# Input projection: the low parts of every other weight unit on GpSimd, and split weights in all units

## The chip, the cores and the metric

The kernel runs on one core of a Trainium2 chip. The metric is the device time of one execution in microseconds (us); lower is better. Engines are named as the profile names them: PE is TensorE's matmul, PEld its weight load, DVE is VectorE, ACT is ScalarE, POOL is GpSimd, SP is SyncE, which issues most DMAs. Data lies in SBUF (tiles named `raw`, `wh`, `wl`, `macc`, `big` and so on) or in PSUM (tiles named `ps`), where PE writes its sums.

## The reference

One decoder layer over 256 tokens of 2048 features in float32: a modulated RMSNorm, a mixer (gated short convolution beside gated linear attention, GLA) and a gated feed-forward part, each with a residual. The change lies in the first product of the mixer, the input projection `h @ w_in`:

```
mod = (c_act @ w_mod[l] + b_mod[l])[:, None, :]
sh_m, sc_m, g_m, sh_f, sc_f, g_f = jnp.split(mod, 6, axis=-1)
h = rmsnorm(x, mix_pre_w[l]) * (1 + sc_m) + sh_m
proj = h @ w_in                                   # (256, 2048) @ (2048, 6160)
cb, cc, cx, q, k, v, r, a_lr = jnp.split(proj, splits, axis=-1)
```

The last 16 columns, `a_lr`, have a path of their own. The other 6144 columns are 48 tiles of 128.

## The kernel before, in words

**Split products.** PE multiplies operands of type fp32r at a short time each and float32 operands at a longer one. To keep the precision of float32, each weight block `raw` is split in two fp32r tiles: ACT copies it into the high part `wh` (`high`, line 138, the copy at line 140), and DVE subtracts that from the block to make the low part `wl` (`low`, line 143, the subtraction at line 145). The activations are split in the same way. A product is then three matmuls: high by high, high by the activation's low part, low by high (lines 490, 491, 492).

**Whole weights.** A unit whose number stands in `FULL`, `FULL1`, `FULL2` or `PLAIN` does without the split: PE multiplies `raw` by the unsplit activations in float32, one matmul for each product (line 487). Before the change these are units 5, 9 and 13 of the last chunk (`FULL`, line 44).

**Chunks and units.** The 16 tiles of the contraction are cut into chunks of 2, 4, 5 and 5 (`CHUNKS`, line 25), so that the projection can begin before the whole modulation is there. In each chunk `in_units` (line 450) makes a list of units of work. In chunks 0 and 1 there are 12 units of 4 column tiles. In chunks 2 and 3 there are 18: units 0 to 3, 6 to 11, 15 and 16 have 3 column tiles, units 4, 5, 12, 13, 14 and 17 have 2. A unit's weight block is 128 partitions by 2048 elements in chunk 1, and by 1920 (3 tiles) or 1280 (2 tiles) in chunks 2 and 3. A unit has `prep` (the load of `raw`, issued by SP, and ACT's high part), `lows` (DVE's low part), `mm` (the matmuls) and `fin`, which adds the finished PSUM banks to the projection's tiles on DVE (`evac`, line 405; line 416, and line 414 by the helper at line 136 for q).

**The order.** `drive` (line 69) writes out the order of all units, and every engine runs its own instructions in that order. While unit i is multiplied, `prep` of unit i+2 and `lows` of unit i+1 have just been issued; then come the sums of unit i-1. `raw` has 6 buffers, `wh` and `wl` have 3 each (`NRAW`, `NHI`, `NLO`, lines 47 to 49). Between these steps stand the steps of the modulation (`mod_steps`, line 157): SP loads a slice of `w_mod`, and DVE multiplies it by a scalar and adds it to an accumulator (line 184, by the helper at line 136). The first step of each accumulator has POOL clear it (line 170) and load the bias row (line 171); it stands ahead of `prep` in unit 9 of chunk 1 (for chunk 3's modulation), in unit 7 of chunk 2 (the mixer's gate) and in unit 4 of chunk 3 (for the feed-forward part). From the last chunk on, the steps of the linear attention stand between the units too; on DVE they are among others lines 611 to 627, 647 and 668.

**POOL.** Before the change it clears accumulators, issues small loads, turns the masks into bytes (line 250, in unit 2 of chunk 2) and adds two residual pieces at the end (line 925).

Of the kernel before, what the change touches and what calls it, by code (L numbers as in the profile page):

```python
# [6 lines left out]
F32 = mybir.dt.float32  # L7
F32R = mybir.dt.float32r
# [6 lines left out]
P = 128  # L15
# [10 lines left out]
PLAIN = ()  # L26
# [14 lines left out]
CONV = (9, 12, 13, 15)  # L41
MODS = (10, 21, 31, 46, 70)
F2_AT = (70, 75, 16)
FULL = (5, 9, 13)
FULL1 = ()
FULL2 = ()
NRAW = 6
NHI = 3
NLO = 3
# [54 lines left out]
def layer_kernel(ctx: ExitStack, tc, x, c, w_mod, b_mod, mix_pre_w, mix_post_w, w_in, conv_w, gate_w2, gate_b,  # L104
                 gla_norm_w, w_out, ffn_pre_w, ffn_post_w, w_up, ffn_conv_w, w_down, ident_in, masks_in, out):
    nc = tc.nc
# [6 lines left out]
    wts = ctx.enter_context(tc.tile_pool(name="wts", bufs=2))  # L113
# [5 lines left out]
    def nm(s):  # L119
        uid[0] += 1  # L120
        return f"{s}_{uid[0]}"
# [4 lines left out]
    def bank(shape):  # L126
        return psp.tile(shape, F32, tag="ps", name=nm("ps"))
# [4 lines left out]
    def raw_tile(shape):  # L132
        return wts.tile(shape, F32, tag="raw", name=nm("raw"), bufs=NRAW)
# [4 lines left out]
    def high(raw, shape):  # L138
        hi = wts.tile(shape, F32R, tag="wh", name=nm("wh"), bufs=NHI)
        nc.scalar.copy(hi, raw)  # L140
        return hi

    def low(raw, hi, shape):
        lo = wts.tile(shape, F32R, tag="wl", name=nm("wl"), bufs=NLO)
        nc.vector.tensor_sub(lo, raw, hi.bitcast(F32))  # L145
        return lo

# [189 lines left out]
    def rstd_of(ss, n, name):  # L337
        r = std_of(ss, n, name)
        nc.vector.reciprocal(r, r)
        return r  # L340
# [9 lines left out]
    def norm_squares(t, name):  # L350
        ss = small.tile([P, 4], F32, tag=name + "ss", name=nm(name))
        for h in range(4):
            square_sum(xs[t][h // 2][:, (h % 2) * 512:(h % 2 + 1) * 512], ss[:, h:h + 1])
        return ss
# [50 lines left out]
    def evac(ci, pair, ps):  # L405

        name = names[pair // 2]
        if name not in proj:
            proj[name] = slot([P, 4, T])
        dst = proj[name][:, (pair % 2) * 2:(pair % 2) * 2 + 2, :]  # L410
        if ci == 0:
            nc.scalar.activation(dst, ps, AF.Copy, scale=QS if name == "q" else 1.0)
        elif name == "q":
            stt(dst, ps, QS, dst)
        else:
            nc.vector.tensor_add(dst, dst, ps)  # L416
# [33 lines left out]
    def in_units(ci):  # L450
        k0, n = bounds[ci], CHUNKS[ci]
        if n <= 4:
            groups = [tuple(range(g, g + 4)) for g in list(range(24, 48, 4)) + list(range(0, 24, 4))]
        else:
            groups = [tuple(range(g, g + 3)) for g in (24, 27, 30, 33)] + [(36, 37), (38, 39)]
            for o, m in ((0, 3), (3, 3), (6, 2)):
                groups += [tuple(range(g + o, g + o + m)) for g in (8, 16, 0)]
            groups += [(40, 41, 42), (43, 44, 45), (46, 47)]
        banks = {}

        def unit(tiles, plain):
            m = len(tiles)
            cur = {}

            def prep():
                r = raw_tile([P, n, m * P])
                nc.sync.dma_start(r, w_in[k0 * P:(k0 + n) * P, tiles[0] * P:(tiles[-1] + 1) * P]
                                  .rearrange("(k p) n -> p k n", p=P))
                cur["w"] = (r,) if plain else (high(r, [P, n, m * P]),)
                cur["r"] = r  # L470

            def lows():
                if not plain:
                    cur["w"] += (low(cur["r"], cur["w"][0], [P, n, m * P]),)

            def mm():
                w = cur["w"]
                for o, nt in enumerate(tiles):
                    if nt // 2 not in banks:
                        banks[nt // 2] = bank([P, 2, T])  # L480
                    ps = banks[nt // 2][:, nt % 2, :]
                    cs = slice(o * P, (o + 1) * P)
                    for kk in range(n):
                        k = k0 + kk
                        st, sp = kk == 0, kk == n - 1
                        if plain:
                            nc.tensor.matmul(ps, w[0][:, kk, cs], h32[ci][k], start=st, stop=sp)  # L487
                        else:
                            ht = hts[k // 2]
                            nc.tensor.matmul(ps, w[0][:, kk, cs], ht[:, k % 2, 0, :], start=st, stop=False)  # L490
                            nc.tensor.matmul(ps, w[0][:, kk, cs], ht[:, k % 2, 1, :], start=False, stop=False)  # L491
                            nc.tensor.matmul(ps, w[1][:, kk, cs], ht[:, k % 2, 0, :], start=False, stop=sp)  # L492

            def fin():
                for nt in tiles:
                    if nt % 2 == 1:
                        evac(ci, nt // 2, banks[nt // 2])

            return Unit(prep, lows, mm, [fin])

        return [unit(g, i in (PLAIN, FULL1, FULL2, FULL)[ci]) for i, g in enumerate(groups)]


    mts = {}
# [252 lines left out]
    def out_units(nh):  # L757
# [5 lines left out]
        def unit(k2):  # L763
# [9 lines left out]
            def lows():  # L773
                cur["w"] += (low(cur["r"], cur["w"][0], [P, 2, 1024]),)
# [89 lines left out]
    def up_units(og, ks, mode):  # L864
# [4 lines left out]
        def unit(k0):  # L869
# [8 lines left out]
            def lows():  # L878
                cur["w"] += (low(cur["r"], cur["w"][0], [P, 4, 512]),)
# [123 lines left out]
    for j, f in enumerate(steps0):  # L1003
# [5 lines left out]
        if j in NLD:  # L1009
            t = NLD.index(j)  # L1010
            r = rstd_of(norm_squares(t, f"n1{t}"), 4, f"n1{t}")
# [12 lines left out]
    for f in modulate_chunk(0, ash, early):  # L1024
        f()

    chunks = [in_units(ci) for ci in range(len(CHUNKS))]
    outs = [out_units(nh) for nh in range(2)]
    owait = outs[0] + outs[1]
# [6 lines left out]
    for ci in range(1, len(CHUNKS)):  # L1036
        n, us = CHUNKS[ci], chunks[ci - 1]
# [312 lines left out]
```

## Time and profile before

| what | value |
|---|---|
| median of 3 runs | 1216.56 us (1216.52 to 1217.66) |
| the profiled execution's own time | 1216.94 us |
| its span, first to last instruction | 1215.1 us |
| time of that execution outside the span | 1.84 us |
| granted TensorE clock, mean | 0.997 |
| chunk 1 of the projection | 76.9 to 151.8 us |
| chunk 2 | 151.8 to 244.2 us |
| chunk 3 | 244.2 to 358.4 us |

The profile gives for each engine its busy time, the groups of its instructions with their number and mean duration, the idle time ahead of them and what ended it. A row of the timeline has start, duration, engine, line, operation, output and inputs. Matmuls overlap in PE's pipeline, so the step from one start to the next is what a matmul costs, not its duration. One float32 matmul of line 487 is shown as two records.

### The profile page before, as it was taken

To read this page: it belongs to the slowest core of one execution; us is meant where nothing else is said; L and a number is where in the kernel's file an instruction comes from. 1 tells how busy PE (TensorE), PEld (TensorE's weight loads), DVE (VectorE), ACT (ScalarE), POOL (GpSimd) and SP (SyncE) were. 2 spreads that over 40 slices of the span, in tenths; PEclk is the share of its full clock that TensorE was granted. 3 is DMA by queue.
4 is the path that set the end of the run, shared out by engine and by line. 5 is a ranking of instruction groups with operands and counts; after the bars stand their busy time and mean duration, and the time that the engine had idled before them with its cause. 6 is when DMAs were issued, how large, how long until landed. Compare 5 with 4: busy or idle time off the path is not lost.

```text
span 1215.1 us, 17130 instructions
## 1 busy us (share of the span) xinstructions
PE 1178.0 (97%) x7003; PEld 1040.8 (86%) x7003; DVE 946.2 (78%) x968; ACT 570.4 (47%) x662; POOL 34.7 (3%) x52
## 2 busy tenths in 40 slices
PE   2999999999999999999999999999999999999997
PEld 1999999999997888888888888888888888888885
DVE  5899999999999886984598979698876665444463
ACT  5563422443474446444554545544544543433452
POOL 2000020000001001000000000000000000000000
PEclk9999999999999999999999999999999999999999
DMA  9999899996699886996667767767664665555522
GB/s 305 386 385 388 310 360 391 398 346 213 201 339 368 321 339 222 361 347 218 237 208 242 257 227 235 251 221 267 223 229 155 239 252 182 207 180 201 194 84 70
DMA packets 128046, 320.73 MB, mean 264 GB/s; under 512 B 8341, under 2 KB 35685, under 8 KB 118240
## 3 DMA queue, kind: packets, MB, share of 16 engines
q1 hardware_dynamic: 125360, 312.63, 72.5%
q0 software_dynamic: 2320, 6.94, 1.6%
q8 instruction: 55, 0.90, 0.3%
q14 instruction: 23, 0.19, 0.0%
q10 hardware_dynamic: 288, 0.07, 0.0%
HBM read 315.42 MB, written 4.19 MB: 263 GB/s over the span
## 4 chain that ended last, share of the span: by engine, by line
PE 91%; DVE 4%; DMA 3%; issue 1%; ACT 1%; SPq 0%; DVEq 0%; ACTq 0%
PE ps L897 27%; PE ps L899 14%; PE ps L753 9%; PE ps L754 9%; PE ps L755 9%; PE ps L490 6%; PE ps L492 6%; PE ps L491 6%; DMA raw<-in_w_mod_dram 2%; PE ps L585 1%; PE ps L487 1%; DVE wl L145 1%; PE ps L282 1%; DVE big L136 1%; DVE macc L136 1%
## 5 line engine op out<-in xcount | busy, mean ns | idle before, releaser
L140 ACT CAST wh<-raw 128x2048 fp32r<-128x2048 f32 (+3 forms) x202 | 366.1, 1815 | 507.7 <-PE ps L897 195.3
L145 DVE TENSOR_TENSOR wl<-raw,wh 128x2048 fp32r<-128x2048 f32 (+3 forms) x202 | 437.1, 2166 | 141.8 <-ACT wh L140 141.8
L897 PE MATMUL ps<-big,wh 128*128 128x512 f32 x1400 | 494.8, 398 | 0.0
L899 PE MATMUL ps<-big,wl 128*128 128x256 f32 x1400 | 393.2, 281 | 1.1 <-DVE wl L145 1.1
L897 PEld LDWEIGHTS ps<-big,wh 128*128 128x128 f32 x1400 | 263.0, 188 | 64.7
L899 PEld LDWEIGHTS ps<-big,wl 128*128 128x128 f32 x1400 | 264.5, 189 | 1.5 <-DVE wl L145 1.5
L492 PE MATMUL ps<-big,wl 128*128 128x256 f32 x733 | 209.8, 286 | 2.7 <-DVE wl L145 2.7
L490 PE MATMUL ps<-big,wh 128*128 128x256 f32 x733 | 211.4, 288 | 0.2 <-ACT wh L140 0.2
L491 PE MATMUL ps<-big,wh 128*128 128x256 f32 x733 | 209.4, 286 | 0.0
L136 DVE SCALAR_TENSOR_TENSOR macc<-raw,c_act,macc 128x2048 f32<-128x2048 f32 (+1 forms) x96 | 199.2, 2075 | 3.0 <-DMA raw<-in_w_mod_dram 2.8
L753 PE MATMUL ps<-wh,big 128*128 128x512 f32 x456 | 178.4, 391 | 0.0
L754 PE MATMUL ps<-wl,big 128*128 128x512 f32 x456 | 177.5, 389 | 0.0
L755 PE MATMUL ps<-wh,big 128*128 128x512 f32 x456 | 177.5, 389 | 0.0
L492 PEld LDWEIGHTS ps<-big,wl 128*128 128x128 f32 x733 | 142.6, 195 | 3.6 <-DVE wl L145 3.6
L490 PEld LDWEIGHTS ps<-big,wh 128*128 128x128 f32 x733 | 142.7, 195 | 2.7 <-ACT wh L140 1.4
L491 PEld LDWEIGHTS ps<-big,wh 128*128 128x128 f32 x733 | 142.8, 195 | 0.1
L755 PEld LDWEIGHTS ps<-wh,big 128*128 128x128 f32 x456 | 85.6, 188 | 17.9
L754 PEld LDWEIGHTS ps<-wl,big 128*128 128x128 f32 x456 | 85.6, 188 | 17.9 <-issue 0.2
L753 PEld LDWEIGHTS ps<-wh,big 128*128 128x128 f32 x456 | 85.6, 188 | 17.9 <-issue 0.2
L136 DVE SCALAR_TENSOR_TENSOR big<-big,fcw,big 128x254 f32<-128x254 f32 (+1 forms) x176 | 72.1, 474 | 0.0
L823 DVE TENSOR_TENSOR big<-big,ps 128x256 f32<-128x256 f32 x88 | 31.1, 415 | 48.4 <-ACT big L821 48.4
L416 DVE TENSOR_TENSOR big<-big,ps 128x512 f32<-128x512 f32 x66 | 43.1, 676 | 0.6 <-PE ps L492 0.5
(199 smaller groups left out, 668.9 us busy)
## 6 DMA issues: line engine op xcount, KB each, us to landing
raw<-in_w_up_dram SPq DMA_DIRECT2D x88, 1024.0 KB, 5.4
raw<-in_w_mod_dram SPq DMA_DIRECT2D x64, 1024.0 KB, 6.8
raw<-in_w_down_dram SPq DMA_DIRECT2D x44, 1024.0 KB, 4.8
raw<-in_w_in_dram SPq DMA_DIRECT2D x24, 960.0 KB, 8.1
raw<-in_w_mod_dram SPq DMA_DIRECT2D x32, 640.0 KB, 7.3
raw<-in_w_out_dram SPq DMA_DIRECT2D x16, 1024.0 KB, 6.9
raw<-in_w_in_dram SPq DMA_DIRECT2D x12, 1024.0 KB, 8.2
raw<-in_w_mod_dram SPq DMA_DIRECT2D x22, 512.0 KB, 6.9
```

The costliest lines, as they stand in the source:

```text
L136: nc.vector.scalar_tensor_tensor(o, a, s, b, op0=op0, op1=op1)
L140: nc.scalar.copy(hi, raw)
L145: nc.vector.tensor_sub(lo, raw, hi.bitcast(F32))
L416: nc.vector.tensor_add(dst, dst, ps)
L490: nc.tensor.matmul(ps, w[0][:, kk, cs], ht[:, k % 2, 0, :], start=st, stop=False)
L491: nc.tensor.matmul(ps, w[0][:, kk, cs], ht[:, k % 2, 1, :], start=False, stop=False)
L492: nc.tensor.matmul(ps, w[1][:, kk, cs], ht[:, k % 2, 0, :], start=False, stop=sp)
L753: nc.tensor.matmul(ps, a[:, i, 0, ts_], w[0][:, kk, ns], start=st, stop=False)
L754: nc.tensor.matmul(ps, a[:, i, 0, ts_], w[1][:, kk, ns], start=False, stop=False)
L755: nc.tensor.matmul(ps, a[:, i, 1, ts_], w[0][:, kk, ns], start=False, stop=sp)
L897: nc.tensor.matmul(pss[o], wh[:, kk, cs], h2[k // 2][:, k % 2, :, :], start=(first and kk == 0), stop=False)
L899: nc.tensor.matmul(pss[o][:, 1, :], wl[:, kk, cs], h2[k // 2][:, k % 2, 0, :], start=False, stop=(last and kk == 3))
```

## The change

In chunks 1, 2 and 3 the units with odd numbers are set aside: their low part is computed by POOL, and it is issued in `prep`, right behind the high part, not in `lows`. The tile of the low part is asked for in `prep` in all units, one unit sooner than before; DVE's subtractions of the even units, and those of all units of chunk 0, stay where they were. `FULL` is empty, so units 5, 9 and 13 of chunk 3 have split weights too; all three are odd, and their low parts fall to POOL.

```
-FULL = (5, 9, 13)
+FULL = ()
...
-    def low(raw, hi, shape):
-        lo = wts.tile(shape, F32R, tag="wl", name=nm("wl"), bufs=NLO)
+    def low_tile(shape):
+        return wts.tile(shape, F32R, tag="wl", name=nm("wl"), bufs=NLO)
+
+    def low(raw, hi, shape, lo=None):
+        lo = low_tile(shape) if lo is None else lo
         nc.vector.tensor_sub(lo, raw, hi.bitcast(F32))
         return lo
...
-        def unit(tiles, plain):
+        def unit(tiles, plain, aside):
...
                 cur["r"] = r
+                if not plain:
+                    cur["l"] = low_tile([P, n, m * P])
+                    if aside:
+                        nc.gpsimd.tensor_sub(cur["l"], r, cur["w"][0].bitcast(F32))
+                        cur["w"] += (cur["l"],)
 
             def lows():
-                if not plain:
-                    cur["w"] += (low(cur["r"], cur["w"][0], [P, n, m * P]),)
+                if not plain and not aside:
+                    cur["w"] += (low(cur["r"], cur["w"][0], [P, n, m * P], cur["l"]),)
...
-        return [unit(g, i in (PLAIN, FULL1, FULL2, FULL)[ci]) for i, g in enumerate(groups)]
+        return [unit(g, i in (PLAIN, FULL1, FULL2, FULL)[ci], ci > 0 and i % 2 == 1) for i, g in enumerate(groups)]
```

Counted out, the units set aside are 6 of 2048 elements in chunk 1, and in chunks 2 and 3 together 12 of 1920 and 6 of 1280: 24 units, of which 21 had a low part on DVE before.

## The prediction

> **What bounds the kernel now.** I began with the page: the span, the busy times and the slices.
>
> ```profile
> span 1215.1 us, 17130 instructions
> PE 1178.0 (97%) x7003; PEld 1040.8 (86%) x7003; DVE 946.2 (78%) x968; ACT 570.4 (47%) x662; POOL 34.7 (3%) x52
> DVE  5899999999999886984598979698876665444463
> POOL 2000020000001001000000000000000000000000
> ```
>
> PE works through nearly the whole span. POOL is all but empty, and DVE is full from the third slice to the twelfth, which is the input projection. The table by stage, with chunks 1, 2 and 3 as windows, is sharper (busy time, with the number of instructions in brackets):
>
> ```profile
> core 0: us, PE busy (x) PEld busy (x) DVE busy (x) ACT busy (x) POOL busy (x), PEclk, DMA share, GB/s
> 76.90:151.80 74.90, 74.90 (x617) 73.37 (x616) 72.10 (x61) 30.48 (x26) 1.58 (x3) 1.00 0.98 357
> 151.80:244.20 92.40, 92.35 (x761) 90.69 (x760) 90.57 (x71) 32.03 (x26) 8.89 (x5) 1.00 1.03 383
> 244.20:358.40 114.20, 113.72 (x870) 110.10 (x870) 111.52 (x122) 59.28 (x96) 1.91 (x4) 1.00 0.77 270
> ```
>
> PE stands idle for 0.05 + 0.48 = 0.5 us of these 281.5 us; DVE is busy for 72.10 + 90.57 + 111.52 = 274.2 and idle for 7.3. So PE sets the end, with DVE right behind it. How close, the timeline shows at chunk 2's unit 15: ACT's high part, DVE's queue, and PE's first matmul of the unit.
>
> ```profile
> 216.78 1.80 ACT L140 CAST wh<-raw 128x1920 fp32r<-128x1920 f32 x1 [2.33 <-DVE macc L136]
> ```
> ```profile
> 219.29 2.34 DVE L136 SCALAR_TENSOR_TENSOR macc<-raw,c_act,macc 128x2048 f32<-128x2048 f32 x1
> 221.56 0.68 DVE L416 TENSOR_TENSOR big<-big,ps 128x512 f32<-128x512 f32 x1
> 222.15 2.15 DVE L145 TENSOR_TENSOR wl<-raw,wh 128x1920 fp32r<-128x1920 f32 x1
> ```
>
> ```profile
> 223.90 0.28 PE L490 MATMUL ps<-big,wh 128*128 128x256 f32 x1
> ```
>
> The low part is ready at 224.30, later than PE begins the unit: here DVE has no reserve left. Work added to DVE's chain is paid by PE from here on; work taken off pays PE almost nothing, since its waits are 0.5 us.
>
> **PE's part of the change.** The whole-weight products of unit 5, and split ones a little later:
>
> ```profile
> 273.46 4.48 PE L487 MATMUL ps<-hf,raw 128*128 128x256 f32 x20
> 277.78 1.95 PE L585 MATMUL ps<-big,big 128*128 128x128 f32 x16
> 279.92 0.28 PE L490 MATMUL ps<-big,wh 128*128 128x256 f32 x1
> 280.04 0.28 PE L491 MATMUL ps<-big,wh 128*128 128x256 f32 x1
> 280.16 0.28 PE L492 MATMUL ps<-big,wl 128*128 128x256 f32 x1
> 280.28 0.28 PE L490 MATMUL ps<-big,wh 128*128 128x256 f32 x1
> ```
>
> Ten products take 277.78 - 273.46 = 4.32 us, 0.432 each; a split one takes 280.28 - 279.92 = 0.36. Units 5, 9 and 13 have 2 + 3 + 2 tiles by 5 = 35 products: 35 x 0.072 = 2.5 us less on PE, a gain as long as PE is the bound. ACT gets three more high parts; it is busy for 59.28 of 114.20 us there, so they are hidden.
>
> **What DVE gives up and POOL takes.** DVE's groups in 76.9 to 358.4 us, and POOL's over the span:
>
> ```profile
> L145 DVE TENSOR_TENSOR wl<-raw,wh 128x1920 fp32r<-128x1920 f32 x23 | 49.4, 2147 | 0.0
> L416 DVE TENSOR_TENSOR big<-big,ps 128x512 f32<-128x512 f32 x63 | 41.2, 676 | 0.6 <-PE ps L492 0.5
> L145 DVE TENSOR_TENSOR wl<-raw,wh 128x2048 fp32r<-128x2048 f32 x12 | 27.3, 2278 | 0.0
> L145 DVE TENSOR_TENSOR wl<-raw,wh 128x1280 fp32r<-128x1280 f32 x10 | 14.8, 1478 | 0.0
> L668 DVE COPY_PREDICATED big<-masks,ps 128x512 f32<-128x512 uint8 x10 | 6.7, 725 | 0.0
> L136 DVE SCALAR_TENSOR_TENSOR big<-ps,big 128x512 f32<-128x512 f32 x8 | 5.2, 672 | 0.0
> ```
> ```profile
> L170 POOL MEMSET macc<- 128x2048 f32 x4 | 7.3, 1816 | 15.4 <-PE ps L306 15.4
> L925 POOL TENSOR_TENSOR big<-big,big 128x512 f32<-128x512 f32 x2 | 2.6, 1281 | 228.8 <-ACT big L924 228.8
> L170 POOL MEMSET big<- 128x1024 f32 x1 | 1.0, 971 | 0.0
> macc<-in_b_mod_dram POOLq DMA_DIRECT2D x4, 8.0 KB, 3.9
> ```
>
> DVE loses 6 x 2.278 + 11 x 2.147 + 4 x 1.478 = 43.2 us. POOL has no subtraction of this size before, so its price is an estimate. Clearing 2048 and 1024 elements takes 1816 and 971 ns, 0.825 ns an element and 0.126 us fixed. The two-operand addition of 512 takes 1281 ns, with the same fixed part 2.26 ns an element. So 2048, 1920 and 1280 elements come to 4.75, 4.46 and 3.02 us; the 24 units to 6 x 4.75 + 12 x 4.46 + 6 x 3.02 = 100.1 us. Ends: 38.5 us at the clearing's pace (43,008 elements), 107.6 us with no fixed part (1281 / 512 = 2.50 ns). I take 100.1: it comes from the nearest row, an operation of the same kind. The Trainium skill, page "GPSIMD Engine Reference", section "Performance versus the Vector engine", gives 4497 ns for a two-input operation of 2048 elements; by that the 24 units would be 94 us, an estimate, and the sum below 6 us less.
>
> **Do the two run side by side?** This decides. The only POOL instruction that reads SBUF while DVE is in its stretch of work is the masks' cast:
>
> ```profile
> 154.30 1.53 DVE L136 SCALAR_TENSOR_TENSOR macc<-raw,c_act,macc 128x1280 f32<-128x1280 f32 x1
> 154.37 4.23 POOL L250 CAST masks<-big 128x768 uint8<-128x768 f32 x1 [4.59 <-DMA big<-in_masks_dram]
> 155.77 2.14 DVE L145 TENSOR_TENSOR wl<-raw,wh 128x1920 fp32r<-128x1920 f32 x1
> 157.84 0.67 DVE L136 SCALAR_TENSOR_TENSOR big<-ps,big 128x512 f32<-128x512 f32 x1
> 158.44 1.53 DVE L136 SCALAR_TENSOR_TENSOR macc<-raw,c_act,macc 128x1280 f32<-128x1280 f32 x1
> ```
>
> It took 4.23 us for 768 elements, 5.5 ns each. Two DVE instructions with both operands in SBUF run back to back beside it, to 157.91; then comes one with an operand from PSUM, and the cast ends at 158.60, 0.69 us later. At the clearing's pace 768 elements need 0.76 us. It looks as if the cast had stood still until the two-operand instructions were through. The other sight of POOL's additions is at the end, where DVE reads PSUM:
>
> ```profile
> 1200.32 2.07 DVE L136 SCALAR_TENSOR_TENSOR big<-ps,rz,big 128x512 f32<-128x512 f32 x3
> ```
> ```profile
> 1201.13 1.30 POOL L925 TENSOR_TENSOR big<-big,big 128x512 f32<-128x512 f32 x1 [221.91 <-ACT big L924]
> ```
>
> Neither is slowed: 2.07 us for three, against 0.67 for one such row above. So I take it that a POOL subtraction and a DVE instruction with two SBUF operands exclude each other, and one with a PSUM operand does not. What no row shows is what POOL does to DVE when it is in first: nothing at one end, DVE shut out for the whole subtraction at the other. I take the second, because an exclusion that DVE holds for whole instructions is most simply held by POOL in the same way. The Trainium skill, page "SBUF — State Buffer", section "Who interferes with whom", states just that: the later of the two "fully blocks". It speaks against this change; the cast agrees with the half that it can show.
>
> **The sum.** POOL gets in when DVE comes to sums from PSUM (L416, L136 with `ps`, L668): 41.2 + 5.2 + 6.7 = 53.1 us over 48 units, 1.11 us for each. One such stretch covers the beginning of a subtraction: 24 x 1.11 = 26.5 us. The rest holds DVE up: 100.1 - 26.5 = 73.6, against the 43.2 given up: 30.4 us more in DVE's chain. Its 7.3 us of idle time take that up as far as they go: 23.1 us are left, and in this stage DVE's delay is PE's.
>
> **Waits on POOL's queue.** The low part now stands on POOL one unit earlier than it stood on DVE, and each first step of an accumulator (clear, bias load) stands behind it. Before, for the gate's accumulator, with ACT's high part of chunk 2's unit 7 and DVE's first step:
>
> ```profile
> 158.55 1.80 POOL L170 MEMSET macc<- 128x2048 f32 x1
> 160.64 0.49 POOL L171 DMA_DIRECT2D macc<-in_b_mod_dram  x1 [0.29 <-POOL macc L170]
> ```
> ```profile
> 177.18 1.80 ACT L140 CAST wh<-raw 128x1920 fp32r<-128x1920 f32 x1 [1.79 <-PE ps L491]
> ```
> ```profile
> 184.03 2.34 DVE L136 SCALAR_TENSOR_TENSOR macc<-raw,c_act,macc 128x2048 f32<-128x2048 f32 x1
> ```
>
> The bias landed at about 160.6 + 3.9 = 164.5, 19.5 us ahead of its use. Now the clearing waits for the subtraction of unit 7, which cannot start before 178.98: 178.98 + 4.46 + 1.80 + 0.29 + 3.9 = 189.4, 5.4 us after DVE wants it; DVE's later low parts are queued behind that, and PE behind them. There are three such places (units 9, 7 and 4 of chunks 1, 2 and 3), so 0 to 16 us. I take 3 us once: a DVE held up by the same subtraction arrives later itself, by its sum and step in hand (0.68 + 2.34), 6.0 - 3.0 = 3.0, and only at unit 7 do I count on no reserve.
>
> The other small loads on POOL (gate, masks, GLA's clearing) are wanted many units later and cost nothing. The low tile asked for sooner costs nothing either: its ring has three buffers like that of the high part, so its writer waits for the same matmuls as the high part ahead of it. A late subtraction also keeps `raw`, and with it SP's next load and all loads behind that; six buffers cover it, and if they don't, it adds to a delay that is there already.
>
> In all 23.1 + 3.0 = 26.1 us. PE's 2.5 us are not taken off, since PE then waits. The profiled execution would come to 1216.94 + 26.1 = 1243.0; the median lies 0.4 us below that execution: 1242.7.
>
> **Rivals.**
>
> *No exclusion (not slower).* The cast is slow in itself, and POOL subtracts beside DVE. For it: no DVE row is lengthened beside POOL, and 5.5 ns an element could be the price of making bytes. Against it: that the cast ends 0.7 us behind the last two-operand instruction would be chance. DVE then loses 43.2 us for nothing in return; POOL is in time even at unit 15 (218.58 + 4.46 = 223.04, PE at 223.9), and the waits on POOL's queue fall into DVE's new reserve. PE saves 2.5, and its 0.5 us of waits go: 1216.56 - 3.0 = 1213.6. This decides as soon as POOL's rows run beside DVE's two-operand rows with both at their usual lengths.
>
> *POOL gives way and DVE is never held up.* As in the cast, POOL moves only in DVE's PSUM stretches, its idle time and what it gave up: 53.1 + 7.3 + 43.2 = 103.6 us, just enough for 100.1. On the average nothing is late, but single low parts are: a pair of units offers some 2 x 1.11 + 2.15 + 0.3 = 4.7 us for one of 4.46, so it takes nearly the two units for which the high part is ahead. If a third of the 24 comes 1 us late, that is 8 us less the 2.5 saved: 1222; 1214 to 1230.
>
> *Nothing is covered.* POOL gets in only where DVE stands still: 100.1 - 43.2 - 7.3 = 49.6 us, 1266.2. Against it: the cast ended beside an instruction with a PSUM operand.
>
> **How the numbers follow.** A measurement of this kernel tells 0.2% (2.4 us) from no change. Forecast 0.52: exclusion both ways. No exclusion 0.24; of that 0.18 is over 2.4 us faster and 0.06 inside, for its gain of 3.0 is hardly over the bound. POOL gives way 0.15: 0.03 faster, 0.04 inside, 0.08 slower. Nothing covered 0.09. So faster 0.18 + 0.03 = 0.21, same 0.06 + 0.04 = 0.10, slower 0.52 + 0.08 + 0.09 = 0.69. The range must hold the case of no exclusion, from 1213, and goes up to 1266, where nothing is covered and the other terms stand; dearer POOL work and what lies under 1213 are left out. The likeliest case alone: 1228 (subtractions at 2.0 ns an element, 11 us less, and no queue wait) to 1256 (with all 16 us of queue waits).
>
> **What would show it.** Line 487 is gone, and lines 490 to 492 have 768 instructions each. POOL has 24 subtractions with about 100 us of busy time if they are held up little, more if they wait inside. Right: DVE's rows at lines 145 and 136 with two SBUF operands have lengths of 4 us and over beside POOL's subtractions, or gaps of that size ahead of them; PE's idle time in chunks 1 to 3 rises from 0.5 to some 25 us, ended by `wl` of DVE or POOL. The prediction is wrong if DVE's rows keep their lengths and PE's idle time stays under a few us; if POOL's subtractions are long (8 us) and DVE's rows are not, POOL gives way.

## The result and the profile after

The changed kernel takes 1275.53 us (median of 4 runs, 1274.70 to 1276.54) against 1217.11 us for the kernel before in the same comparison: a ratio of 1.0477 (95% interval 1.0463 to 1.0491), 58 us slower. The forecast had the sign, 1242.7 us and a range up to 1266; the loss is more than twice the forecast's 26 us and lies outside the range. The lines of the new kernel have moved: DVE's subtraction is line 148, POOL's 477, PE's products of the projection 498 to 500 (768 matmuls each, as counted ahead), the accumulators' clearing and bias load 173 and 174.

The page of the profile after begins so (the slices are tenths of busy time, 40 over the span; PEclk is the granted TensorE clock):

```profile
span 1274.8 us, 17215 instructions
PE 1189.4 (93%) x7038; PEld 1050.4 (82%) x7038; DVE 979.8 (77%) x947; ACT 574.3 (45%) x665; POOL 147.6 (12%) x76
...
DVE  5879978998999978698469897879796764444454
POOL 2034344334322000100000000000000000000000
PEclk9999898989899999999999999999999999999999
```

DVE has 21 subtractions fewer and is yet busy for 33.6 us longer than before (946.2). POOL works in slices 3 to 13, the three chunks with units set aside, and only among those does the granted clock fall to 0.8, in four of them. The table by stage, for chunks 1, 2 and 3 of the kernel after, in the columns of the table in the prediction:

```profile
75.70:163.00 87.30, 78.38 (x618) 75.76 (x617) 79.06 (x56) 31.25 (x26) 38.19 (x9) 0.94 0.80 290
163.00:283.20 120.20, 99.56 (x761) 96.82 (x760) 104.04 (x63) 32.06 (x26) 43.42 (x16) 0.91 0.87 315
283.20:417.20 134.00, 116.68 (x905) 113.84 (x905) 124.99 (x116) 62.45 (x98) 45.41 (x14) 0.96 0.64 227
sum 341.50, PE 294.62 PEld 286.42 DVE 308.10 ACT 125.77 POOL 127.02; mean PE 98.21 PEld 95.47 DVE 102.70 ACT 41.92 POOL 42.34
```

The chunks take 341.5 us instead of 281.5: 60.0 us more, which is the whole loss (the span grew by 59.7). A stage is as long as DVE's busy and idle time together. Busy time rose from 274.2 to 308.1, by 33.9; idle time from 7.3 to 341.5 - 308.1 = 33.4, by 26.1. These are two different losses. The forecast has nearly all of the first and next to none of the second.

**The first: DVE is shut out.** DVE's and then POOL's timeline of the kernel after, around one subtraction (start, duration, engine, line):

```profile
124.54 2.29 DVE L148 TENSOR_TENSOR wl<-raw,wh 128x2048 fp32r<-128x2048 f32 x1
126.74 5.91 DVE L136 SCALAR_TENSOR_TENSOR macc<-raw,c_act,macc 128x1280 f32<-128x1280 f32 x1
132.57 1.27 DVE L419 TENSOR_TENSOR big<-big,ps 128x512 f32<-128x512 f32 x2
133.77 1.54 DVE L136 SCALAR_TENSOR_TENSOR macc<-raw,c_act,macc 128x1280 f32<-128x1280 f32 x1
```
```profile
125.04 6.26 POOL L477 TENSOR_TENSOR wl<-raw,wh 128x2048 fp32r<-128x2048 f32 x1 [7.21 <-ACT wh L140]
131.24 1.16 POOL L173 MEMSET macc<- 128x1280 f32 x1
```

POOL's subtraction begins, by its row, at 125.04, inside a subtraction of DVE's that runs its usual 2.29 us. DVE's next instruction takes 5.91 us, the same instruction 7 us later 1.54. It ends at 132.65, 1.35 us after POOL's subtraction has ended at 131.30: it stood still until POOL was through. So the subtraction shuts DVE out for its whole length. It does not wait for a stretch of sums from PSUM, as the prediction had it; it gets in as soon as the one running instruction ends. By their lengths 23 of the 24 subtractions waited for no more than that; the one at 264.47 took 5.21 us instead of the shortest 2.88 and let a second DVE instruction through first. DVE's sums from PSUM keep their mean of 676 ns (63 of them before, 63 after), and the one at 202.48 takes 0.68 us in the middle of a subtraction: they run beside POOL, as the prediction read it.

**The second: DVE waits.** DVE's waits for the modulation's loads in the three chunks of the kernel before, then its two largest in the kernel after, then PE's (us in total, times, longest):

```profile
DVE macc L136 <- DMA raw<-in_w_mod_dram: 1.3, 2, 1.1
```
```profile
DVE macc L136 <- DMA raw<-in_w_mod_dram: 14.0, 9, 3.8
DVE macc L136 <- issue: 11.6, 3, 5.1
```
```profile
PE ps L500 <- DVE wl L148: 26.9, 8, 8.8
...
PE ps L500 <- POOL wl L477: 5.2, 4, 2.5
```

The 11.6 us are first steps of accumulators: the three places of the prediction's "Waits on POOL's queue". The second of them, with POOL's queue, DVE and PE in this order:

```profile
201.27 5.45 POOL L477 TENSOR_TENSOR wl<-raw,wh 128x1920 fp32r<-128x1920 f32 x1 [8.57 <-ACT wh L140]
206.65 1.82 POOL L173 MEMSET macc<- 128x2048 f32 x1
208.76 0.50 POOL L174 DMA_DIRECT2D macc<-in_b_mod_dram  x1 [0.29 <-POOL macc L173]
213.78 4.23 POOL L477 TENSOR_TENSOR wl<-raw,wh 128x1920 fp32r<-128x1920 f32 x1 [4.51 <-ACT wh L140]
```
```profile
207.99 0.67 DVE L419 TENSOR_TENSOR big<-big,ps 128x512 f32<-128x512 f32 x1
213.77 6.38 DVE L136 SCALAR_TENSOR_TENSOR macc<-raw,c_act,macc 128x2048 f32<-128x2048 f32 x1 [5.11 <-issue]
220.08 2.14 DVE L148 TENSOR_TENSOR wl<-raw,wh 128x1920 fp32r<-128x1920 f32 x1
```
```profile
213.16 0.28 PE L499 MATMUL ps<-big,wh 128*128 128x256 f32 x1
222.28 0.58 PE L500 MATMUL ps<-big,wl 128*128 128x256 f32 x1 [8.84 <-DVE wl L148]
```

The clearing stands behind the subtraction and the bias load behind the clearing. DVE has nothing it may do from 208.66 to 213.77. Then POOL's next subtraction starts beside it and the step takes 6.38 us instead of 2.34; behind that stands the low part for which PE has waited since 213.44, 8.84 us in all.

The 14.0 us are late weights of the modulation, and those come from SP. Its waits for POOL in the three chunks, of which there were none before:

```profile
SPq L470 <- POOL wl L477: 94.3, 13, 10.9
...
SPq L179 <- POOL wl L477: 55.4, 7, 13.7
...
SPq L776 <- POOL wl L477: 6.1, 2, 3.7
```

SP stands for 94.3 + 55.4 + 6.1 = 156 us behind a `raw` buffer that a subtraction of POOL's still reads, and every load of the queue with it. SP's waiting is not a loss in itself: it stood for some 240 of the 281.5 us in the kernel before too, for readers on DVE and PE, and stands for some 297 of 341.5 now. It costs where a load comes late for its reader, as with the 14.0 us. The loads had little in hand: the DMA share, 0.98 and 1.03 in chunks 1 and 2 before, is 0.80 and 0.87 now. That a held load could not be made up for this reason is likely, but no run tests it.

### The profile page after: what moved, and what is told of

The parts are those of the page before. It is cut to its first block, busy times and chain, and to the rows that moved or that the text cites. A ratio compares the mean times of both kernels' runs of the same rounds, so it can differ in the third digit from the quotient of the medians.

```text
span 1274.8 us, 17215 instructions
## 1 busy us (share of the span) xinstructions
PE 1189.4 (93%) x7038; PEld 1050.4 (82%) x7038; DVE 979.8 (77%) x947; ACT 574.3 (45%) x665; POOL 147.6 (12%) x76
## 4 chain that ended last, share of the span: by engine, by line
PE 72%; DVE 9%; DMA 8%; issue 4%; POOL 3%; ACT 2%; SPq 0%; DVEq 0%; POOLq 0%; ACTq 0%
PE ps L905 25%; PE ps L907 13%; PE ps L762 9%; PE ps L763 9%; PE ps L761 9%; DMA raw<-in_w_in_dram 4%; DMA raw<-in_w_mod_dram 4%; POOL wl L477 3%; DVE wl L148 2%; PE ps L500 2%; PE ps L498 2%; PE ps L499 2%; DVE macc L136 2%; DVE big L136 2%; ACT wh L140 1%
## 5 line engine op out<-in xcount | busy, mean ns | idle before, releaser
L140 ACT CAST wh<-raw 128x2048 fp32r<-128x2048 f32 (+3 forms) x205 | 370.4, 1810 | 544.3 <-PE ps L905 195.3
L148 DVE TENSOR_TENSOR wl<-raw,wh 128x2048 fp32r<-128x2048 f32 (+3 forms) x181 | 403.7, 2232 | 145.6 <-ACT wh L140 141.8
L907 PE MATMUL ps<-big,wl 128*128 128x256 f32 x1400 | 393.2, 281 | 1.1 <-DVE wl L148 1.1
L905 PEld LDWEIGHTS ps<-big,wh 128*128 128x128 f32 x1400 | 263.0, 188 | 64.9
L136 DVE SCALAR_TENSOR_TENSOR macc<-raw,c_act,macc 128x2048 f32<-128x2048 f32 (+1 forms) x96 | 246.6, 2569 | 26.8 <-DMA raw<-in_w_mod_dram 15.0
L907 PEld LDWEIGHTS ps<-big,wl 128*128 128x128 f32 x1400 | 264.5, 189 | 1.5 <-DVE wl L148 1.5
L500 PE MATMUL ps<-big,wl 128*128 128x256 f32 x768 | 224.3, 292 | 35.4 <-DVE wl L148 30.1
L498 PE MATMUL ps<-big,wh 128*128 128x256 f32 x768 | 224.8, 293 | 0.2 <-ACT wh L140 0.2
L499 PE MATMUL ps<-big,wh 128*128 128x256 f32 x768 | 222.3, 289 | 0.0
L500 PEld LDWEIGHTS ps<-big,wl 128*128 128x128 f32 x768 | 152.4, 198 | 39.1 <-DVE wl L148 33.0
L498 PEld LDWEIGHTS ps<-big,wh 128*128 128x128 f32 x768 | 152.7, 199 | 2.7 <-ACT wh L140 1.4
L499 PEld LDWEIGHTS ps<-big,wh 128*128 128x128 f32 x768 | 152.7, 199 | 0.0
L477 POOL TENSOR_TENSOR wl<-raw,wh 128x1920 fp32r<-128x1920 f32 (+2 forms) x24 | 116.5, 4855 | 265.0 <-ACT wh L140 253.9
```

What stands on the lines that cost most here:

```text
L136: nc.vector.scalar_tensor_tensor(o, a, s, b, op0=op0, op1=op1)
L477: nc.gpsimd.tensor_sub(cur["l"], r, cur["w"][0].bitcast(F32))
L905: nc.tensor.matmul(pss[o], wh[:, kk, cs], h2[k // 2][:, k % 2, :, :], start=(first and kk == 0), stop=False)
L907: nc.tensor.matmul(pss[o][:, 1, :], wl[:, kk, cs], h2[k // 2][:, k % 2, 0, :], start=False, stop=(last and kk == 3))
```

## The experiments

Two theories stood against each other first. Mine: the loss is the exclusion of the two engines, plus waits on POOL's queue, plus `raw` held too long. The rival: POOL is only slow and its low parts come late, or the granted clock does it. Each time below is a median, with its ratio to the kernel before in the same comparison (1216.8 to 1217.8 us) and the 95% interval.

**POOL writes only** (write_only): the 24 low tiles are made by POOL in the same places and in about the same order of time, but without reading SBUF beyond one element. The low parts of these units are left out.

```
-                        nc.gpsimd.tensor_sub(cur["l"], r, cur["w"][0].bitcast(F32))
...
+                        nc.gpsimd.tensor_copy(one, cur["w"][0][:, 0, 0:1].bitcast(F32))
...
+                        for e in (slice(0, None), slice(0, None), slice(0, half)):
+                            nc.gpsimd.memset(flat_l[:, e], 0.0)
```

> The changed kernel, but POOL computes no low part in the units set aside: it reads one element of the high part and then clears the tile of the low part two and a half times, which takes about as long (4.6, 4.3 and 2.9 us by the rate of its clearing) but reads nothing. The low parts of these 24 units are left out of the result. Queue places, buffers and waits are those of the changed kernel. Theory (the exclusion of POOL's reading and DVE's two-operand instructions): no DVE row is lengthened, the 74.7 us by which 24 DVE rows are too long go, DVE has 43 us less to do than before, and what is left are the waits on POOL's queue: 1214 to 1226 us. Rival (POOL's low parts, and the loads behind them, are late because POOL takes 4 to 6 us each): 1255 us or more.

It took 1224.45 us, 1.0049 (1.0032 to 1.0066). DVE's two groups of accumulator steps in the three chunks, in the kernel before, in the kernel after and then in this one (busy us, mean ns), and the sum row of this run's table by stage:

```profile
L136 DVE SCALAR_TENSOR_TENSOR macc<-raw,c_act,macc 128x2048 f32<-128x2048 f32 x25 | 58.6, 2342 | 1.3 <-DMA raw<-in_w_mod_dram 1.3
L136 DVE SCALAR_TENSOR_TENSOR macc<-raw,c_act,macc 128x1280 f32<-128x1280 f32 x29 | 44.7, 1540 | 0.2
```
```profile
L136 DVE SCALAR_TENSOR_TENSOR macc<-raw,c_act,macc 128x2048 f32<-128x2048 f32 x25 | 77.6, 3106 | 10.4 <-issue 10.1 <-DMA raw<-in_w_mod_dram 0.4
L136 DVE SCALAR_TENSOR_TENSOR macc<-raw,c_act,macc 128x1280 f32<-128x1280 f32 x29 | 72.9, 2514 | 15.4 <-DMA raw<-in_w_mod_dram 13.7 <-issue 1.6
```
```profile
L136 DVE SCALAR_TENSOR_TENSOR macc<-raw,c_act,macc 128x2048 f32<-128x2048 f32 x25 | 58.7, 2347 | 15.4 <-DMA macc<-in_b_mod_dram 7.8 <-issue 5.8 <-DMA raw<-in_w_mod_dram 1.8
L136 DVE SCALAR_TENSOR_TENSOR macc<-raw,c_act,macc 128x1280 f32<-128x1280 f32 x29 | 44.9, 1548 | 14.0 <-DMA raw<-in_w_mod_dram 8.1 <-issue 5.8
```
```profile
sum 289.10, PE 280.66 PEld 275.11 DVE 233.28 ACT 125.46 POOL 123.31; mean PE 93.55 PEld 91.70 DVE 77.76 ACT 41.82 POOL 41.10
```

2514 and 3106 ns are back at 1548 and 2347, with POOL nearly as busy as in the kernel after (123.3 us in the stage, against 127.0). DVE's busy time is 233.3 us, where the prediction's 274.2 - 43.2 makes 231.0. A POOL that is merely busy or late does not lengthen DVE's rows; a POOL that reads its operands from SBUF does. DVE has idle time here too, 289.1 - 233.3 = 55.8 us, and waits for the bias load are among it.

**The clearing issued earlier** (early_clear): clearing and bias load of the three accumulators go to POOL's queue some units ahead, before the subtraction that they stood behind.

```
...
+    for i, key in ((11, (0, bounds[3] * P)), (25, (2, 0)), (43, (3, 0))):
+        allin[i].early.insert(0, clears[key])
```

> The changed kernel, but the clearing and the bias load of three accumulators stand on POOL's queue some units earlier (in units 11 of chunk 0, 1 of chunk 2, 1 of chunk 3), so that no subtraction set aside stands between them and their use. Theory (the waits on POOL's queue are a cost of their own): DVE's three long waits in the changed kernel, 1.6 + 5.1 + 5.0 = 11.6 us, go, and most of that comes off the time: 1264 to 1268 us. Rival (DVE is held up by the subtractions anyhow, and the waits only fall into that): the three waits go and others grow, 1274 to 1277 us.

1263.81 us, 1.0381 (1.0356 to 1.0406): 12 us come back, about the 11.6 of the three waits, as the theory had it (the time is 0.2 us under its interval). The sum row of its table by stage:

```profile
sum 330.40, PE 295.21 PEld 286.25 DVE 310.19 ACT 127.36 POOL 124.72; mean PE 98.40 PEld 95.42 DVE 103.39 ACT 42.45 POOL 41.57
```

DVE's busy time is what it was (310.2); its idle time is 330.4 - 310.2 = 20.2 instead of 33.4.

**Both together** (write_early): POOL writes only, and the clearing comes early. Low parts left out again.

> The last two edits together: POOL only writes (the low parts of the 24 units set aside are left out of the result), and the three accumulators are cleared and their bias loaded ahead of the subtractions' places. Theory (exclusion and the waits on POOL's queue are the two costs, and without them the change does what it is for): 1212 to 1216 us, at or under the kernel before. Rival (a third cost, loads held back by POOL or the slower clock, is there without them too): 1220 us or more.

1215.66 us, 0.9977 (0.9963 to 0.9991): with no queue wait and no reading by POOL, of `raw` in particular, nothing of the loss is left.

**Halves** (halves): each of POOL's subtractions in two, so that DVE gets in between.

```
-                        nc.gpsimd.tensor_sub(cur["l"], r, cur["w"][0].bitcast(F32))
+                        for e in (slice(0, m * P // 2), slice(m * P // 2, m * P)):
+                            nc.gpsimd.tensor_sub(cur["l"][:, :, e], r[:, :, e], cur["w"][0][:, :, e].bitcast(F32))
```

> The changed kernel, but each subtraction on POOL is made in two, half of the columns each. Theory on record (POOL gets in only beside DVE's sums from PSUM, and one such stretch covers the beginning of each instruction): twice as many beginnings are covered, DVE is held up for 74.7 - 26 = 49 us, and the time falls to about 1250 us. Rival (POOL gets in as soon as the DVE instruction that runs has ended, whatever it reads): the sum of what DVE is held up stays at 70 to 80 us, in 48 pieces, and the time at 1270 to 1280 us.

1278.02 us, 1.0497 (1.0478 to 1.0517). DVE's busy time fell to 288.9, so it was held for 288.9 - 231.0 = 57.9 us and not 77. The rival had the time right, but not its reason: the hold did shrink. Nothing was gained, for POOL itself needs longer (154.5 us busy, against 127.0), and DVE's idle time rose to 343.9 - 288.9 = 55.0 us. With the early clearing as well (halves_early):

> Each subtraction in two halves, and the early clearing. With halves alone DVE was held up 20 us less, and stood idle 22 us more. Theory (part of that idle time are the three waits on POOL's queue, 18.8 us there, since halves take longer to get through): 1256 to 1262 us, under the early clearing alone by some us. Rival (halves are no gain: what DVE is not held up, POOL is late): 1264 to 1270 us.

1261.64 us, 1.0371 (1.0336 to 1.0406), not to be told from early_clear's 1.0381. What DVE wins by being let in, it gives back as waits.

**Whole weights kept** (full_kept): `FULL = (5, 9, 13)` as before, 21 units set aside.

> The low parts on POOL alone: units 5, 9 and 13 of chunk 3 keep their whole weights, so 21 units are set aside. Theory (each subtraction holds DVE up for some 3 us, and those three give DVE nothing back): 9 to 11 us less DVE time in chunk 3, 2.5 us more on PE: 1264 to 1270 us. Rival (chunk 3 is bound by the linear attention's chain and not by DVE's time): 1275 to 1279 us.

1261.69 us, 1.0364 (1.0342 to 1.0386), 14 us less than the kernel after and 2 us under the theory's interval; chunk 3 takes 119.1 us instead of 134.0. DVE's busy time there is 9.7 us less, as the theory had it; besides, the third of the queue waits went, 5.0 us, which the kernel after has in this chunk.

**The other part alone** (no_whole): `FULL` is empty, the low tile is asked for sooner, and no unit is set aside.

> The other part of the change alone: no unit has whole weights, and all low parts are made by DVE. DVE has 1.48 + 2.15 + 1.48 = 5.1 us more to do in chunk 3, PE 2.5 us less. Theory (DVE has 2 to 9 us in hand in most of chunk 3, so PE's gain stands): 1214 to 1216 us. Rival (the reserve is 1.6 to 2.5 us in the last units, so PE waits there): 1217 to 1220 us.

1220.00 us, 1.0023 (1.0014 to 1.0033). The rival of this run was right: PE's 2.5 us were not to be had, because DVE, which now makes all low parts (278.2 us busy), sets the end.

**Only these three on POOL** (only_three):

> POOL makes the low parts of units 5, 9 and 13 of chunk 3 alone, those that had whole weights; all others stay on DVE. Theory (each subtraction holds DVE up for 2 to 4 us, some 9 us in all, against a reserve of 2 to 9 us, and PE has 2.5 us less): 1218 to 1224 us, no better than with these three on DVE. Rival (DVE's reserve in chunk 3 takes it up): 1213 to 1216 us, better than the kernel before.

1231.60 us, 1.0119 (1.0103 to 1.0135), worse than either theory had it. Chunk 3 of no_whole and of only_three:

```profile
243.50:359.60 116.10, 113.42 (x905) 111.16 (x905) 114.47 (x124) 61.90 (x98) 1.84 (x4) 0.99 0.76 262
```
```profile
246.20:371.70 125.50, 115.30 (x905) 112.98 (x904) 117.52 (x121) 61.87 (x98) 17.14 (x8) 0.96 0.70 242
```

Three subtractions on POOL instead of DVE cost 9.4 us in this chunk (the medians are 11.6 apart). DVE is busy for 3.1 us more although it lost three subtractions, and idle for 8.0 instead of 1.6; one wait of 5.04 us for the bias of the feed-forward's accumulator is the largest part.

**What holds SP** took four runs. First a mere hold (write_hold): write_only, with one element of `raw` read by POOL behind its writing, so that `raw` is kept till POOL is done with the unit.

> POOL only writes, as in the run with that edit alone, but behind its writing it reads one element of the weight block, so that the block is held as long as by a subtraction that is not held up (the low parts of the 24 units are left out). Theory (SP's loads come late because POOL holds the weight block longer than DVE did): DVE and ACT wait for loads more, 1228 to 1235 us. Rival (six buffers cover it, and the loads of the changed kernel are late only because the subtractions are): 1221 to 1227 us.

1228.06 us, 1.0087 (1.0072 to 1.0102): 3.6 us over write_only, at the lower edge of what the theory expected. POOL also has one more instruction for each unit here (139.1 us busy, against 123.3), so these 3.6 us are not the hold alone. SP stands behind POOL for 96 us in this run: where DVE is not full (295.1 - 236.1 = 59.0 us idle), they cost 3.6 us at most. The other way round (early_no_hold): early_clear, but POOL subtracts the high part from itself and never reads `raw`; the low parts of these units are left out.

> The run with the early clearing, but POOL subtracts the high part from itself: two operands in SBUF as before, so the exclusion stays, but the weight block is free for SP's next load as soon as ACT has copied it (the low parts of the 24 units are left out). Theory (of the 58 us, what is left beside DVE's being held up and the waits on POOL's queue is the late loads, behind blocks that POOL holds): 1252 to 1258 us. Rival (the loads are late because all else is): 1261 to 1266 us, as with the early clearing alone.

1235.06 us, 1.0155 (1.0137 to 1.0173), far below what was expected, and not for one reason. POOL's 24 subtractions in the kernel after and in this one (shortest, median, longest in ns):

```profile
L477 POOL TENSOR_TENSOR wl<-raw,wh x24: 2880/5290/6260, 76.6 to 402.6; 128x1920 fp32r<-128x1920 f32 x12, 128x2048 fp32r<-128x2048 f32 x6, 128x1280 fp32r<-128x1280 f32 x6
```
```profile
L484 POOL TENSOR_TENSOR wl<-wh x24: 2417/3994/5727, 80.2 to 364.7; 128x1920 fp32r<-128x1920 f32 x12, 128x2048 fp32r<-128x2048 f32 x6, 128x1280 fp32r<-128x1280 f32 x6
```

The subtraction with one tile for both operands is itself shorter, so DVE is held for less (289.5 us busy, against 310.2), beside idle time that fell from 20.2 to 9.1. The three chunks are 31.8 us shorter than early_clear's, 20.7 of them busy time and 11.1 idle time. The second figure is what one would put down to the free `raw`: SP waits for POOL nowhere, and DVE's waits for its loads are 2.5 us instead of early_clear's 14.1. But the shorter subtractions bear on it too; the run does not tell the two apart cleanly.

Then the place of the issue (at_lows): POOL's subtraction is issued in `lows`, one unit later, where DVE's stood; the tile is still asked for in `prep`.

```
                     cur["l"] = low_tile([P, n, m * P])
-                    if aside:
-                        nc.gpsimd.tensor_sub(cur["l"], r, cur["w"][0].bitcast(F32))
-                        cur["w"] += (cur["l"],)
 
             def lows():
+                if not plain and aside:
+                    nc.gpsimd.tensor_sub(cur["l"], cur["r"], cur["w"][0].bitcast(F32))
+                    cur["w"] += (cur["l"],)
```

> The changed kernel, but POOL's subtraction is issued where DVE's was, one unit later (only the tile is asked for sooner). Theory (a subtraction takes up to 6 us with its wait, so it needs the unit's head start): PE waits for POOL's low parts, which it does for 5 us in all in the changed kernel: 1280 to 1300 us. Rival (POOL's queue is empty when the high part is ready, so it starts at the same time): 1273 to 1278 us.

Both theories were wrong: 1256.72 us, 1.0333 (1.0306 to 1.0359), 19 us faster than the kernel after. POOL begins its first subtraction at the same time in both (76.6 and 76.5 us), since both wait for the high part. What changed first is SP's queue. SP's issues from 71 to 84 us in the kernel after and in at_lows:

```profile
71.28 2.02 SPq L179 DMA_DIRECT2D raw<-in_w_mod_dram  x2
82.29 0.37 SPq L470 DMA_DIRECT2D raw<-in_w_in_dram  x1
```
```profile
71.15 2.03 SPq L179 DMA_DIRECT2D raw<-in_w_mod_dram  x2
75.01 0.37 SPq L470 DMA_DIRECT2D raw<-in_w_in_dram  x1
```

It is the load of the same weight unit, 7.3 us apart. Which buffer of `raw` a load gets does not go by which comes free first. In the kernel after, this load gets the one that POOL's first subtraction reads, and waits till that ends (82.26); the load behind it, at 82.71, waits for nothing more. With the subtraction issued one unit later, the same load gets a buffer that a subtraction of DVE's frees at 74.98. One reading is a turn, in which the buffer whose last reader was issued first is next. These two kernels fit that, but write_hold does not: there POOL reads the block at the same early place, and yet the same load is let go by DVE, at 74.84, and the next one by POOL, at 85.27. So the place of the issue moves the turn, and the rule behind the turn stays open. SP's waits for POOL in at_lows:

```profile
SPq L179 <- POOL wl L479: 54.9, 11, 7.9
...
SPq L470 <- POOL wl L479: 26.3, 5, 8.8
...
SPq L776 <- POOL wl L479: 6.1, 2, 3.7
```

87 us instead of 156. The later issue moves more than the loads, though: the clearings now stand ahead of the subtractions that they stood behind. DVE's idle time is 18.5 us less than in the kernel after; its queue waits, 11.6 before, are 3.8, and its waits for the loads, 14.0 before, are 7.1. With both edits, the later issue and the early clearing (lows_early):

> The two edits that were tried singly, together: POOL's subtraction is issued where DVE's was, one unit later, so that its weight block is handed to a later load; and the three accumulators are cleared and their bias loaded some units earlier. Theory (the prediction's sum for the exclusion holds, 30 us in DVE's chain and 23 on the time, and what it left out are the waits on POOL's queue and the loads behind blocks that POOL holds): DVE is held up for 70 to 76 us as before, its idle time falls from 33 us to 7 to 12, and the time to 1240 to 1250 us. Rival (the two edits cure the same waits, and the exclusion itself costs twice the forecast): 1253 to 1258 us, like the later subtraction alone.

1251.45 us, 1.0282 (1.0268 to 1.0296), 1.5 us above the theory's interval; DVE's hold, 303.15 - 231.0 = 72.2 us, and its idle time of 11.9 lie inside theirs. The sum rows of at_lows and of lows_early:

```profile
sum 321.80, PE 294.31 PEld 286.48 DVE 306.95 ACT 127.90 POOL 125.07; mean PE 98.10 PEld 95.49 DVE 102.32 ACT 42.63 POOL 41.69
```
```profile
sum 315.00, PE 292.45 PEld 284.75 DVE 303.15 ACT 124.84 POOL 124.65; mean PE 97.48 PEld 94.92 DVE 101.05 ACT 41.61 POOL 41.55
```

DVE's idle time is 14.9 in the one and 11.9 in the other, against 33.4 in the kernel after. The two edits bring 24 us together and 12 + 19 = 31 singly; at_lows alone had already shortened the queue waits. What the later issue brings without them is read from early_clear against lows_early: 1263.81 - 1251.45 = 12.4 us. What is left over the kernel before is 33.5 us in the stage: 29.0 us of DVE's busy time and 4.5 us of idle time. Of the versions with all of the computation, none came below the kernel before.

**The clock** (fillers): 184 matmuls without use, in PE's longest waits of chunks 1 and 2, keep the granted clock of these two chunks at 1.00, where the kernel after has 0.94 and 0.91. Chunk 3 has none.

> The changed kernel, with matmuls without use ahead of four units whose low part is late (46 in unit 10 of chunk 1; 36, 70 and 32 in units 6, 8 and 14 of chunk 2, 0.12 us each), in a bank that the unit's first product overwrites, so that PE is not idle there. Theory (in those waits the granted clock falls to half, and PE's work behind them is slower by 1.2 to 1.8 us a unit): 5 to 7 us less, 1268 to 1271 us. Rival (DVE sets the pace there, PE's slower work is hidden): 1273 to 1278 us.

1272.25 us, 1.0456 (1.0439 to 1.0473), between the two theories: 3 us less, with an interval that overlaps that of the kernel after. The clock is not the cause of the loss; whether it has a part of some 3 us stays open.

## Why the prediction was off

**The bound: right.** PE and DVE were both full; work put on DVE's chain was paid by PE. PE's idle time in the chunks rose from 0.5 to 341.5 - 294.6 = 46.9 us ("some 25" was forecast), and the largest part of it ends with DVE's `wl`.

**POOL's prices: right.** The shortest subtractions of the kernel after take 4.71, 4.23 and 2.88 us for 2048, 1920 and 1280 elements; the estimates were 4.75, 4.46 and 3.02. The means below are longer because POOL's span begins while it still waits for DVE's running instruction:

```profile
L477 POOL TENSOR_TENSOR wl<-raw,wh 128x1920 fp32r<-128x1920 f32 x12 | 61.1, 5092 | 120.6 <-ACT wh L140 109.5 <-issue 11.0
L477 POOL TENSOR_TENSOR wl<-raw,wh 128x2048 fp32r<-128x2048 f32 x6 | 33.9, 5644 | 100.0 <-ACT wh L140 100.0
L477 POOL TENSOR_TENSOR wl<-raw,wh 128x1280 fp32r<-128x1280 f32 x6 | 21.6, 3592 | 44.4 <-ACT wh L140 44.4
```

**The exclusion: right in size, wrong in how POOL gets in.** "100.1 - 26.5 = 73.6" of DVE held up; measured 308.1 - 231.0 = 77.1 (74.8 against write_only's own 233.3). That write_only brings DVE's rows back shows the cause. The Trainium skill, page "SBUF — State Buffer", section "Who interferes with whom", has one rule: the port pair that DVE and GpSimd share is an exclusive lock. The rows agree: 5.91 us against 1.54 beside a subtraction, 1.55 beside write_only's clearings. The words "fully blocks", which the prediction quotes, stand in that section of the Trainium skill in the sentence on DVE's 2-port modes; what bears on these instructions is the one rule. But the 26.5 us of cover came from a picture that did not hold. POOL waited for no more than the running instruction in 23 of 24 cases, and is covered by whatever PSUM-fed work or idle time DVE happens to have during its run. That 100.1 - 77.1 = 23.0 us were covered in the end is near the 26.5 by chance.

**The failing step: "Its 7.3 us of idle time take that up as far as they go: 23.1 us are left".** The forecast took DVE's idle time down to the 3.0 us of a queue wait. It was 33.4. The difference of 30.4 us and the 3.5 us of the exclusion make up the stage's miss of 60.0 - 26.1 = 33.9. The 30.4 have three parts.

- *"I take 3 us once" for POOL's queue: measured 11.6.* The mechanism and its three places were right, the size was not. At unit 7 of chunk 2 the wait was 5.11 us and not 3.0: from the subtraction's end at 206.72 the clearing and the bias took 7.05 us and not 6.0, and DVE came 1.94 us behind that end and not 3.0. The other two places, put at nothing because DVE was thought to have a reserve there, cost 1.56 and 4.96. That is 8.6 us too little, and early_clear, which takes the 11.6 away, brings 12.
- *"Six buffers cover it, and if they don't, it adds to a delay that is there already": 14.0 us of DVE's waits for its own loads.* The kernel before has 1.3. The buffers do not cover it, since a load does not get the buffer that is free first, and the early issue made loads wait for POOL's slow subtraction. With the queue waits out of the way in both, moving the issue brings 12.4 us (early_clear against lows_early) and takes these waits from 14.1 to 7.8. A delay on SP's queue came on top of DVE's hold, and did not run beside it.
- *The old idle time was not used up: 33.4 - 11.6 - 14.0 = 7.8 us.* The kernel before has 7.3 - 1.3 = 6.0 us of waits other than for the modulation's loads. They are not simply still there: its largest, 2.5 us for ACT, is gone, and 3.8 us ahead of DVE's own low parts are new, for which the profile names no releaser. In lows_early, with the queue waits gone and 7.8 us of waits for loads left, the others come to 11.9 - 7.8 = 4.1. That a hold delays the inputs of DVE as well as DVE is how I read this; no run took it by itself.

**PE's 2.5 us: rightly left out,** and no_whole shows why more plainly than the prediction had it: with DVE full, splitting three more units costs 2.8 us and saves none. The size was right too: in write_early, where DVE is not full, PE works for 111.1 us in chunk 3 instead of 113.7.

**The clock was not thought of.** With the clock halved in and behind PE's waits, PE's work in the chunks takes 294.6 us instead of 281.0 - 2.5 = 278.5. fillers took away about 8 of these 16 us, those of chunks 1 and 2 (78.38 + 99.56 = 177.9 in the kernel after, and 81.32 + 110.48 - 184 x 0.12 = 169.7), and gained about 3: there most of them lie beside DVE's chain. For chunk 3 no run shows it.

**The rivals.** "No exclusion" and "POOL gives way" fell with the first 5.91 us row. "Nothing is covered" gives 1266.2, nearest to the result, but for a wrong reason: 23 us were covered, and the waits were missing.

## What to carry to other kernels

A two-operand instruction given from VectorE to GpSimd does not free VectorE where VectorE's own instructions have two operands in SBUF: 43.2 us of subtractions were given up, and 77.1 us of standing still came in return. An instruction that moves to another engine takes a place in two more orders, that of the new engine's queue (here the clearings and bias loads behind it) and that in which its input buffer is handed to the next load; look at what stands behind it in both. The idle time of a nearly full engine was no reserve for new work here: it was waiting for inputs, and the new work added waits of its own.

## What was not expected of the hardware

- The masks' cast on POOL, 4226 ns in the kernel before, takes 822 ns in the kernel after, at 187.23 us, where DVE is idle (its last instruction ended at 186.32): it had stood still, as the prediction read it. But it had waited through two back-to-back DVE instructions, whereas the subtraction at 125.04 got in after one; of the 24 only the one at 264.47 let two through. Why some are kept out longer stays open.
- POOL's subtraction with one tile as both operands takes at least 3.76, 3.39 and 2.42 us for 2048, 1920 and 1280 elements, against 4.71, 4.23 and 2.88 with two tiles.
- The granted clock halves soon after PE begins to wait, and stays low after it has resumed. The windows of the kernel after around PE's wait from 213.44 to 222.28 (from 213.00 to 215.50 the clock is still 1.00):

```profile
215.50:225.70 10.20, 3.42 (x16) 3.42 (x17) 10.20 (x5) 1.79 (x1) 2.51 (x1) 0.50 0.76 277
225.70:229.00 3.30, 3.30 (x29) 3.30 (x29) 2.25 (x2) 0.00 (x0) 0.00 (x0) 0.99 1.02 376
```

The clock is 0.50 for 10.2 us, the last 3.4 of which have matmuls. The Trainium skill, page "TensorE: Matmul & The Clock Gate", section "Part 1: The HAM clock gate (the "warmup" mystery)", gives a window of about 3.4 us of sustained work before the full clock returns; the 225.70 - 222.28 = 3.4 us here agree.
